# A new list of steps for the stick-breaking stage, with the adaptive weights visited four tiles at a time

## The chip, the cores and the metric

The kernel runs on one core of a Trainium2 chip. The metric is the device time of one execution in microseconds (us). The time before is 1705.46 us, the median of 3 runs (1704.63 to 1706.43). One execution was profiled; it took 1706.82 us, and its span from first to last instruction is 1704.7 us.

Engine names: PE is the matmul engine (PEld its weight loads), ACT the scalar engine, DVE the vector engine, POOL the general engine, which here mostly issues stores, and SP the engine that issues loads. PE, ACT and DVE each work through their own instructions in the order in which the program lists them; they meet at semaphores only.

## The reference, cut

One layer of a hybrid encoder for 1024 prompt frames and 32 sample frames, in float32. The part that the change touches is the stick-breaking attention (8 heads of 64) and the matmuls that run beside it: the gate projections and the adaptive (ada) vectors.

```python
ada = jax.nn.silu(c) @ w_ada + b_ada            # 1024 -> 6 * 1024, for two rows c
sh1, sc1, gt1, sh2, sc2, gt2 = split(ada, 6)
h = rms_norm(x, g_pre_mix) * (1 + sc1) + sh1
p = h @ w_in                                     # 4256 columns, 2048 of them the two gates
...
def sb_attend(q, qpos, k, v, kpos):
    z = einsum('bqhd,bshd->bhqs', q, k) * SB_SCALE
    mask = kpos[None, :] < qpos[:, None]
    sp = where(mask, softplus(z), 0.0)
    later = cumsum(sp, axis=3, reverse=True) - sp
    a = where(mask, exp(log_sigmoid(z) - later), 0.0)
    return einsum('bhqs,bshd->bqhd', a, v)
...
x = x + gt1 * rms_norm(merged @ w_out, g_post_mix)
h2 = rms_norm(x, g_pre_ffn) * (1 + sc2) + sh2
```

`sh1` and `sc1` are needed before the projection and are made in the first stage. The other four vectors of `ada` (32 weight tiles of 128x1024) are made inside the stick-breaking stage, since nothing needs them sooner.

## The kernel before

The stages follow each other: normalised input (`stage_h`), the q, k, v projections (`stage_qkv`), stick-breaking attention (`stage_sb`), latent projections (`stage_lat`), latent attention, merge, up and down projections. The change lies in `stage_sb`, which the trace shows from 193.01 to 516.87 us.

`stage_sb` makes four passes (`for p in range(4)`, at the end of `stage_sb`), one for each pair of heads. In a pass `sb_attend` walks the list `ORDER` (L691 to L711), written out by hand: each entry issues one piece of work, and the entries of PE, ACT and DVE go to these engines in just that order (`manual_schedule`). So the list decides what stands behind what on each engine. The same list serves all four passes.

An entry is a letter and a place, as in `S2.0a`: here 2 is the unit (four units of 256 query rows for each of two heads, 0 to 7), 0 the first of its two blocks of 128 rows, and a or b the half of the key columns where they are too many for one PSUM bank. The letters:

- `S` (PE): the scores, two matmuls (L1154, L1155) into one of three PSUM banks called `s`.
- `a`, `e`, `l` (ACT): absolute value, exp, log of the scores (L742, L744, L746). `x`, `c`, `k`, `d` (DVE): softplus, the running sum along the keys (a scan, L752 or L755), a copy of its first column, the difference (L748 to L760). `d` is the last to read the bank, so a later `S` in that bank waits for it. `E` (ACT, L762): the final exp.
- `T` (PE, L803): transposes of the weights into one of two banks `tr`; `h` (ACT) and `v` (DVE) copy them out in two parts; `V` (PE, L817): the product with the values; `o` (ACT) and `p` (DVE) copy the result out.
- `f` (PE): the next step of the gate projections, which fill PE while the attention waits for ACT and DVE. Such a step is three matmuls of 128x352 (L75, L76, L77). Eight steps make one block of a gate tile in one of two PSUM banks `mm`, three blocks make a tile, 16 tiles make the gates: four tiles, 96 steps, in each pass.
- `G` (ACT): copy a finished block out of its `mm` bank (L1080); POOL then stores it. `W` (ACT, L68) and `w` (DVE, L71): split the next gate tile's weights in two parts; `W` waits until the load of that tile (`wr`) has landed. The load of tile m+1 is issued when tile m begins.
- `D`, `Q` (DVE): add the ada products to their sum; turn a finished vector.

The ada products are made in `ada_step`. Before, a visit takes two weight tiles and follows the first block of every gate tile (L1064 to L1067), each weight tile being one step `f` of the list; so a pass has 104 `f`, of which 8 are ada tiles. A weight tile takes four matmuls (L236), one for each group of 32 columns of PE's array, into one `mm` bank:

```python
for j in range(4):
    nc.tensor.matmul(ps[32 * j : 32 * j + 32, :256], self.cT[:, k], w[:, j * 256 : j * 256 + 256], ...)
```

After a visit `ada_fetch` issues the loads of the next one's weight tiles. The loads of a pass's q, k and v (`queries`, `values`) are issued beside certain entries (the dictionary `then`: the second head's at `S2.0a` and `S2.1a`, the next pass's first head at `S3.1b` and `V3.0`). All these loads and those of the gate weights go through SP's queue (`load`, L83) in the order of the program. The stores of `stage_qkv` go through POOL's queue and are still under way when `stage_sb` begins.

Of the kernel before, what the change touches and what calls it, by code (L numbers as in the profile page):

```python
# [8 lines left out]
F32 = mybir.dt.float32  # L9
# [8 lines left out]
P = 128  # L18
D = 1024
# [25 lines left out]
class K:  # L45
# [182 lines left out]
    def ada_step(self, n, pool, tp, late):  # L228


        nc, a = self.nc, self.a
        ps = self.bank("mm")
        for i, (v, k) in enumerate(self.ada_todo[:n]):
            w = self.ada_w.pop(0)
            for j in range(4):
                nc.tensor.matmul(ps[32 * j : 32 * j + 32, :256], self.cT[:, k], w[:, j * 256 : j * 256 + 256],  # L236
                                 start=i == 0, stop=i == n - 1)
# [10 lines left out]
        yield  # L248

    def ada_turn(self):  # L250

# [192 lines left out]
    def stage_qkv(self):  # L444
# [249 lines left out]
        f2 l1.1 x2.0a V0.0 E1.0 c2.0a f1 a2.0b o0 f1 x1.1 e2.0b f1 W p0 f1 k2.0a d2.0a l2.0b f1 c1.1 E2.0a f1  # L694
        S2.1a x2.0b G f1 a2.1a d1.1 e2.1a c2.0b f2 E1.1 f1 w l2.1a S2.1b f1 a2.1b x2.1a T1.1 e2.1b T1.0 d2.0b
        h1.1 c2.1a f1 h1.0 f1 l2.1b v1.1 S3.0a E2.0b v1.0 f1 a3.0a f1 k2.1a d2.1a G e3.0a x2.1b V1.1 E2.1a c2.1b
        l3.0a S3.0b V1.0 x3.0a a3.0b o1 f1 p1 T2.2 h2.2 e3.0b d2.1b f1 c3.0a f1 E2.1b f1 l3.0b v2.2 S3.1a k3.0a
        d3.0a T2.1 h2.1 a3.1a x3.0b E3.0a V2.2 f1 c3.0b T2.0 e3.1a S3.1b h2.0 f1 v2.1 l3.1a f1 G v2.0 a3.1b f1
        x3.1a W f1 d3.0b V2.1 c3.1a D V2.0 f1 w o2 S4.0 e3.1b E3.0b f1 a4.0 f1 l3.1b f1 p2 e4.0 k3.1a d3.1a l4.0
        f2 x3.1b E3.1a f1 x4.0 c3.1b f1 G T3.3 c4.0 S4.1 a4.1 T3.2 h3.3 d3.1b f1 e4.1 v3.3 h3.2 f1 d4.0 f1 l4.1  # L700
        E3.1b v3.2 S5.0 f1 E4.0 x4.1 c4.1 a5.0 V3.3 e5.0 V3.2 l5.0 d4.1 T3.1 E4.1 x5.0 T3.0 h3.1 f1 c5.0 h3.0
        S5.1 S6.0a v3.1 a5.1 f1 v3.0 a6.0a T4.0 e5.1 f1 d5.0 h4.0 V3.1 E5.0 v4.0 f1 l5.1 V3.0 G x5.1 S6.0b e6.0a
        f1 o3 c5.1 f1 a6.0b l6.0a e6.0b f1 p3 l6.0b d5.1 f2 x6.0b E5.1 V4.0 x6.0a f1 o4 c6.0a S6.1a T5.1 p4
        a6.1a T5.0 k6.0a d6.0a h5.1 f1 c6.0b e6.1a f1 G h5.0 v5.1 f1 E6.0a v5.0 S6.1b l6.1a f1 W f1 x6.1a d6.0b
        V5.1 V5.0 D c6.1a E6.0b a6.1b S7.0a w o5 f2 e6.1b l6.1b a7.0a f1 k6.1a p5 e7.0a f1 d6.1a x6.1b E6.1a f1
        c6.1b l7.0a S7.0b f1 x7.0a T6.2 a7.0b f1 d6.1b h6.2 c7.0a f1 E6.1b f1 G e7.0b S7.1a v6.2 f1 k7.0a d7.0a
        l7.0b T6.1 T6.0 a7.1a h6.1 V6.2 x7.0b c7.0b h6.0 S7.1b e7.1a f1 v6.1 E7.0a f1 v6.0 l7.1a f1 d7.0b a7.1b
        f1 x7.1a V6.1 E7.0b V6.0 e7.1b c7.1a f1 G o6 l7.1b f1 p6 k7.1a d7.1a x7.1b f2 E7.1a f1 c7.1b f2 T7.3
        d7.1b T7.2 h7.3 f1 h7.2 E7.1b v7.3 f1 G f1 v7.2 f1 V7.3 V7.2 D T7.1 f1 h7.1 v7.1 T7.0 f1 h7.0 v7.0 f1
        V7.1 f2 V7.0 f1 o7 f1 W p7 f1 Q f1 w G f7 G  # L710
    """.split()  # L711

    def sb_attend(self, score, V, out, fill, then):
        nc = self.nc
        act, vec = nc.scalar.activation, nc.vector
        tiles, banks, seen = {}, {}, {}
        common = self.sums(V, out, tiles)
        todo = None
        for x in self.ORDER:
            if todo:  # L720
                todo()
            todo = then.get(x)
            k, x = x[0], x[1:]
            if k in "fGDQWw":
                for _ in range(int(x or 1)):
                    fill(k)
                continue
            h, u = divmod(int(x[0]), 4)
            if k in "SaelxckdE":
                n, i, part = x[0], int(x[2]), x[3:]  # L730
                w = (2 * u + i + 1) * P
                m = w // 2 if part else w
                c0 = m if part == "a" else 0
                if k == "S":
                    if part != "b":
                        tiles[x[:3]] = self.tl(self.At, [P, TP], F32, "A")
                    banks[x] = self.tl(self.ps, [P, 512], F32, "s")
                    score(h, banks[x], 2 * u + i, c0, max(m, 256))
                    continue
                ps, A = banks[x][:, :m], tiles[x[:3]][:, c0 : c0 + m]  # L740
                if k == "a":
                    act(A, ps, AF.Abs)  # L742
                elif k == "e":
                    act(A, A, AF.Exp, scale=-1.0)  # L744
                elif k == "l":
                    act(A, A, AF.Ln, bias=1.0)  # L746
                elif k == "x":
                    vec.scalar_tensor_tensor(A, ps, 0.0, A, ALU.max, ALU.add)  # L748
                elif k == "c":
                    r = A[:, ::-1]  # L750
                    if part == "b":
                        vec.tensor_tensor_scan(r, r, r, seen[x[:3]], ALU.add, ALU.bypass)  # L752
                    else:

                        vec.tensor_tensor_scan(r, self.reset[:, 512 - m : 512][:, ::-1], r, -NEG, ALU.mult, ALU.add)  # L755
                elif k == "k":
                    seen[x[:3]] = self.tl(self.sm, [P, 1], F32, "mn")
                    vec.tensor_copy(seen[x[:3]], A[:, 0:1])
                elif k == "d":
                    vec.tensor_tensor(A, ps, A, ALU.subtract)  # L760
                else:
                    act(A, A, AF.Exp)  # L762
                continue
            common(k, x, h, u)
# [278 lines left out]
    def gates(self):  # L1043
# [7 lines left out]
        def steps():  # L1051
            for m in range(16):
                wh, wl = w.pop(0)
                for b, (c0, n) in enumerate(self.BLK):
                    if b == 0:
                        c = 2208 + (m + 1) * P if m < 15 else 3 * P
                        raw.append(self.wload([(0, 1024, self.a["w_in"][0, :, c : c + P].rearrange("(k p) c -> p k c", p=P), 8)]))
                    ps.append((m, c0, n, self.bank("mm")))
                    for k in range(KT):
                        self.mm3(ps[-1][3][:, :n], wh[:, k], wl[:, k], self.Hh[k][:, c0 : c0 + n],  # L1060
                                 self.Hl[k][:, c0 : c0 + n], k == 0, k == KT - 1)
                        if k < KT - 1:
                            yield
                    if b == 1 and self.ada_sum is not None:  # L1064
                        ada.append(self.ada_turn())
                    yield
                    if b == 0:  # L1067
                        yield from self.ada_step(2, self.sm2, self.Sp, ada)
                        if m == 15:
                            self.sample_load(1)  # L1070

        step = steps()

        def do(kind):
            if kind == "f":
                next(step)
            elif kind == "G":
                m, c0, n, x = ps.pop(0)
                g = self.tl(self.At, [P, 512], F32, "nat")
                nc.scalar.copy(g[:, :n], x[:, :n])  # L1080
# [25 lines left out]
    def stage_sb(self):  # L1106
# [1500 lines left out]
```

## Time and profile before

| what | value |
|---|---|
| median of 3 runs | 1705.46 us |
| the profiled execution, its span | 1706.82 us, 1704.7 us |
| PE busy, DVE busy, ACT busy over the span | 97%, 75%, 58% |
| `stage_sb`, first pass | 85.64 us |
| `stage_sb`, second to fourth pass | 79.41, 79.40 and 79.41 us |
| instructions of `stage_sb` on PE in a pass | some 556 |

A group's row gives line, engine, operation, what is written and read, shape, count, then busy time, mean duration and the idle time before it with what ended it. A timeline row gives the start in us from the span's start, the duration, then the same names; idle time before it stands in brackets. PE's matmuls overlap: a matmul of 128x352 lasts 0.32 us, but the next one starts 0.16 us later, so the cost of a step on PE is the time from start to start.

### The profile page before, as it was taken

Reading aid. Unit: us, or ns where it says so; the run is one execution under the profiler, and the core shown is the slowest. Engines: PE = TensorE matmul, PEld = TensorE weight load, DVE = VectorE, ACT = ScalarE, POOL = GpSimd, SP = SyncE. Lnnn points to the kernel's source line nnn. Section 1 sums busy time; section 2 is a strip of 40 time slices with the busy share of each in tenths; the row PEclk is TensorE's granted clock in tenths of the full one; section 3 lists DMA queues with packets and bytes.
Section 4 is the critical chain, followed back from the end, with each engine's and each line's share of the span. In section 5 each row is a group of like instructions: output and inputs, shape, how many; then the busy total and the mean of one; then the engine's idle time right before and its main releaser. Section 6 shows DMA issues by size and latency. Waiting matters only on the chain. (4 is left out here: it accounts for less than half of the span.)

```text
span 1704.7 us, 30268 instructions
## 1 busy us (share of the span) xinstructions
PE 1660.8 (97%) x11646; PEld 1512.1 (89%) x11646; DVE 1272.9 (75%) x2129; ACT 993.6 (58%) x1945; POOL 292.8 (17%) x569
## 2 busy tenths in 40 slices
PE   5999999999999999999999999999999999999997
PEld 3999889999999898998889789999999999887885
DVE  4865697979783688777766779887787777787456
ACT  4544597978774667777763476444444444544442
POOL 3113311111110221111100221221121111110013
PEclk8999999999999999999999999999999999999999
DMA  9345984647432421222374531433333333697643
GB/s 333 100 133 180 280 250 130 200 117 227 150 104 66 149 79 47 67 68 70 107 238 140 173 131 62 134 104 131 131 104 132 131 108 133 231 331 250 207 139 120
DMA packets 185728, 255.20 MB, mean 150 GB/s; under 512 B 14702, under 2 KB 125056, under 8 KB 185584
## 3 DMA queue, kind: packets, MB, share of 16 engines
q1 hardware_dynamic: 164944, 194.11, 36.5%
q0 software_dynamic: 20416, 59.08, 9.8%
q8 instruction: 91, 1.49, 0.4%
q14 instruction: 53, 0.43, 0.1%
q10 hardware_dynamic: 224, 0.09, 0.0%
HBM read 187.86 MB, written 64.57 MB: 148 GB/s over the span
## 5 line engine op out<-in xcount | busy, mean ns | idle before, releaser
L68 ACT ACTIVATE wh<-wr 128x1024 fp32r<-128x1024 f32 (+5 forms) x163 | 132.2, 820 | 226.3 <-PE s L2061 80.4
L71 DVE TENSOR_TENSOR wl<-wr,wh 128x1024 fp32r<-128x1024 f32 (+5 forms) x163 | 149.9, 928 | 78.0 <-ACT wh L68 77.6
L75 PE MATMUL mm<-hh,wh 128*128 128x352 f32 x456 | 153.0, 336 | 0.0
L76 PE MATMUL mm<-hl,wh 128*128 128x352 f32 x456 | 149.5, 328 | 0.4 <-DVE hl L331 0.3
L77 PE MATMUL mm<-hh,wl 128*128 128x352 f32 x456 | 148.7, 326 | 0.0
L2060 PE MATMUL mm<-T,wh 128*128 128x256 f32 (+1 forms) x376 | 108.1, 288 | 0.0
L2062 PE MATMUL mm<-T,wl 128*128 128x256 f32 (+1 forms) x376 | 107.0, 285 | 0.3 <-DVE wl L71 0.2
L2061 PE MATMUL mm<-T,wh 128*128 128x256 f32 (+1 forms) x376 | 106.7, 284 | 0.0
L2060 PE MATMUL s<-T,wh 128*128 128x256 f32 (+1 forms) x348 | 99.2, 285 | 0.0
L2062 PE MATMUL s<-T,wl 128*128 128x256 f32 (+1 forms) x348 | 99.1, 285 | 0.0
L2061 PE MATMUL s<-T,wh 128*128 128x256 f32 (+1 forms) x348 | 99.0, 284 | 0.0
L71 DVE TENSOR_TENSOR wl<-S,wh 128x1024 fp32r<-128x1024 f32 (+1 forms) x55 | 59.1, 1077 | 49.2 <-ACT wh L68 48.8
L76 PEld LDWEIGHTS mm<-hl,wh 128*128 128x128 f32 x456 | 86.4, 190 | 3.3 <-DVE hl L331 1.8
L75 PEld LDWEIGHTS mm<-hh,wh 128*128 128x128 f32 x456 | 86.4, 190 | 3.2 <-ACT A L762 1.6
L2201 DVE SCALAR_TENSOR_TENSOR u<-u,c,u 128x1058 f32<-128x1058 f32 x68 | 87.0, 1316 | 2.0 <-ACT u L2198 0.7
L77 PEld LDWEIGHTS mm<-hh,wl 128*128 128x128 f32 x456 | 86.5, 190 | 0.2
L803 PE MATMUL tr<-c,A 128*128 128x128 f32 x576 | 84.2, 275 | 0.9 <-DVE A L919 0.3
L68 ACT ACTIVATE wh<-S 128x1024 fp32r<-128x1024 f32 (+1 forms) x55 | 51.8, 943 | 49.5 <-PE s L2061 13.4
L2062 PE MATMUL tr<-T,wl 128*128 128x272 f32 (+1 forms) x272 | 77.6, 285 | 0.2 <-DVE wl L71 0.2
L2060 PE MATMUL tr<-T,wh 128*128 128x272 f32 (+1 forms) x272 | 77.7, 286 | 0.0
L2061 PE MATMUL tr<-T,wh 128*128 128x272 f32 (+1 forms) x272 | 77.3, 284 | 0.0
L71 DVE TENSOR_TENSOR PTl<-tr,PTh 128x512 fp32r<-128x512 f32 x96 | 64.5, 683 | 13.1 <-ACT PTh L68 12.3
(760 smaller groups left out, 5789.2 us busy)
## 6 DMA issues: line engine op xcount, KB each, us to landing
wr<-in_w_up_dram SPq DMA_DIRECT2D x44, 512.0 KB, 4.0
dr<-in_w_down_dram SPq DMA_DIRECT2D x43, 512.0 KB, 5.9
wr<-in_w_in_dram SPq DMA_DIRECT2D x33, 512.0 KB, 5.4
A<-in_w_ada_dram SPq DMA_DIRECT2D x32, 512.0 KB, 7.6
wr<-gdn SPq DMA_DIRECT2D x30, 512.0 KB, 5.0
gdn<-u POOLq DMA_DIRECT2D x23, 512.0 KB, 5.1
gd<-nat POOLq DMA_DIRECT2D x48, 176.0 KB, 4.1
t<-gd SPq DMA_DIRECT2D x16, 528.0 KB, 5.6
```

What stands on the lines that cost most here:

```text
L68: self.nc.scalar.activation(out, in_, AF.Identity, scale=scale)
L71: return self.nc.vector.tensor_tensor(out, full, hi.bitcast(F32), ALU.subtract)
L75: m(ps, lh, rh, start=start, stop=False)
L76: m(ps, lh, rl, start=False, stop=False)
L77: self.pe = m(ps, ll, rh, start=False, stop=stop).ins
L803: self.nc.tensor.transpose(tr[:, (2 * s + q) * P : (2 * s + q + 1) * P], at[q][:, b * P : b * P + P], self.idt)
L2060: m(ps[:, :n], w[0][:, k], x[0][:, k, c], start=first and k == 0, stop=False, skip_group_check=True)
L2061: m(ps[:, :n], w[0][:, k], x[1][:, k, c], start=False, stop=False, skip_group_check=True)
L2062: i = m(ps[:, :n], w[1][:, k], x[0][:, k, c], start=False, stop=k == 3, skip_group_check=True)
L2201: nc.vector.scalar_tensor_tensor(y, u[:, w : w + YW], self.cvT[:, w, cc : cc + 1], y, ALU.mult, ALU.add)
```

## The change

The list `ORDER` is written anew: the same entries of the attention, with other places; 96 `f` in place of 104, two `D` in place of four, and two new entries `A`. The `f` stand closer together at a pass's start and are gone from its end. Its first lines, some from a quarter of the way down, and the last, before and now:

```diff
-        S0.0 S0.1 a0.0 S1.0 a0.1 e0.0 e0.1 l0.0 f2 l0.1 x0.0 a1.0 x0.1 f1 c0.1 c0.0 e1.0 f1 l1.0 f1 d0.0 d0.1
-        E0.0 f1 x1.0 c1.0 E0.1 f1 S1.1 S2.0a a1.1 T0.0 d1.0 f1 G a2.0a h0.0 v0.0 f1 e2.0a f1 e1.1 S2.0b l2.0a D
+        S0.0 a0.0 f1 S0.1 f1 a0.1 e0.0 S1.0 f1 l0.0 f1 e0.1 f1 a1.0 l0.1 e1.0 f1 x0.0 c0.0 f1 d0.0 E0.0 f2 S2.0a
+        x0.1 c0.1 f1 l1.0 f1 a2.0a x1.0 d0.1 c1.0 W f1 e2.0a f1 G l2.0a w x2.0a f1 S1.1 f1 a1.1 f1 E0.1 f2 e1.1
...
-        h1.1 c2.1a f1 h1.0 f1 l2.1b v1.1 S3.0a E2.0b v1.0 f1 a3.0a f1 k2.1a d2.1a G e3.0a x2.1b V1.1 E2.1a c2.1b
-        l3.0a S3.0b V1.0 x3.0a a3.0b o1 f1 p1 T2.2 h2.2 e3.0b d2.1b f1 c3.0a f1 E2.1b f1 l3.0b v2.2 S3.1a k3.0a
+        l2.1b h1.0 c2.1a E2.0a f2 S3.0a x2.1b T1.1 G a3.0a h1.1 k2.1a e3.0a d2.1a f4 v1.0 E2.1a S3.0b l3.0a f1
+        c2.1b f2 v1.1 x3.0a d2.1b V1.1 c3.0a G a3.0b f1 e3.0b S3.1a l3.0b x3.0b E2.0b E2.1b T2.2 k3.0a d3.0a A
+        h2.2 c3.0b V1.0 v2.2 a3.1a d3.0b f1 e3.1a S4.0 l3.1a T2.0 f1 W x3.1a S3.1b o1 T2.1 D E3.0a a3.1b c3.1a G
+        f1 p1 f2 e3.1b f2 w a4.0 f2 k3.1a d3.1a S5.0 h2.1 l3.1b x3.1b V2.2 h2.0 E3.1a f1 e4.0 v2.1 a5.0 T3.3
...
-        V7.1 f2 V7.0 f1 o7 f1 W p7 f1 Q f1 w G f7 G
+        d7.0b h7.3 d7.1b E7.0b f3 E7.1b f1 v7.3 p6 f1 v7.2 T7.1 V7.3 V7.2 h7.1 T7.0 f1 G f1 h7.0 f1 w G v7.1
+        v7.0 V7.1 V7.0 o7 p7
```

An `A` is one visit of four ada tiles at once; two in a pass, so beside every second gate tile. `ada_step` is no longer a generator, and the gates' steps no longer call it:

```diff
             for j in range(4):
                 nc.tensor.matmul(ps[32 * j : 32 * j + 32, :256], self.cT[:, k], w[:, j * 256 : j * 256 + 256],
                                  start=i == 0, stop=i == n - 1)
-            if i < n - 1:
-                yield
...
-            if k in "fGDQWw":
+            if k in "fGDQWwA":
...
                     yield
-                    if b == 0:
-                        yield from self.ada_step(2, self.sm2, self.Sp, ada)
-                        if m == 15:
-                            self.sample_load(1)
...
+            elif kind == "A":
+                self.ada_step(4, self.sm2, self.Sp, ada)
+                if not self.ada_todo:
+                    self.sample_load(1)
```

The first ada tiles are no longer loaded ahead of the first pass, but four at once beside `S2.1a` of the first pass; the buffers of the pool `sm2` are laid out ahead:

```diff
+        for g, w, n in (("big", BIG, 3), ("A", TP, 2)):
+            for _ in range(n):
+                self.tl(self.sm2, [P, w], F32, g)
 
         self.sent = self.wlast
         queries(0, 0)
-        self.ada_w = []
-        self.ada_fetch(2, S)
+        self.ada_w, self.ada_sum = [], None
         values(0, 0)
...
             then = {"S2.0a": lambda: queries(p, 1), "S2.1a": lambda: values(p, 1)}
+            if p == 0:
+                then["S2.1a"] = lambda: (values(p, 1), self.ada_fetch(4, self.sm2))
```

Outside `stage_sb` the three engines' instructions stand as before. Three places where they moved follow, each as the program's own list of instructions before and after (an x4 at a row's end counts equal ones; the changed kernel's line numbers are a few lower).

The first place is PE at the ada visit in the middle of the second pass before, where `A` are the ada weight tiles, `mm` a PSUM bank, `s` scores:

```order
L77 MATMUL mm_2789<-hh_94,wl_2586 128x352
L236 MATMUL mm_2864<-A_2592,cT 32x256 x4
L1154 MATMUL s_2871<-KH_279_2205,Q_278_2204 128x384
L1155 MATMUL s_2871<-KL_277_2203,Q_278_2204 128x384
L236 MATMUL mm_2864<-A_2594,cT 32x256 x4
L75 MATMUL mm_2886<-hh_94,wh_2585 128x352
```

And the first visit of the first pass now:

```order
L800 MATMUL tr_2536<-c_70,A_2387 128x128
L236 MATMUL mm_2543<-A_2392,cT 32x256 x4
L236 MATMUL mm_2543<-A_2394,cT 32x256 x4
L236 MATMUL mm_2543<-A_2396,cT 32x256 x4
L236 MATMUL mm_2543<-A_2398,cT 32x256 x4
L814 MATMUL pv_2514<-PTh_2448,V_285_2216 128x256
```

Two weight tiles that stood apart, or in pairs elsewhere, are now four in a row.

The second place is ACT in the first pass, at the split of the first gate tile that the stage loads (`wh<-wr`, the entry `W`). Before, it is ACT's 24th instruction of the stage and stands behind the first product's copy (`o<-pv`):

```order
L762 ACTIVATE A_2245<-A_2245 128x384
L742 ACTIVATE A_2295<-s_2335 128x320
L789 COPY o_2360<-pv_2349 64x256
L744 ACTIVATE A_2295<-A_2295 128x320
L68 ACTIVATE wh_2370<-wr_2253 128x1024
L746 ACTIVATE A_2295<-A_2295 128x320
```

Now it is the 12th:

```order
L759 ACTIVATE A_2237<-A_2237 128x128
L743 ACTIVATE A_2257<-A_2257 128x384
L739 ACTIVATE A_2292<-s_2293 128x320
L68 ACTIVATE wh_2315<-wr_2242 128x1024
L741 ACTIVATE A_2292<-A_2292 128x320
L1073 COPY nat_2325<-mm_2244 128x352
```

The split moved up by twelve instructions; the copy of the first gate block (`nat<-mm`), which stood well ahead of it, is now behind it.

The third place is SP's queue at the stage's start, before:

```order
L83 DMA KL_286_2217<-kl_546 64x1024 x2
L83 DMA A_2229<-in_w_ada_dram 128x1024
L83 DMA A_2231<-in_w_ada_dram 128x1024
L83 DMA V_285_2216<-vd_550 128x8x128
L83 DMA wr_2253<-in_w_in_dram 128x8x128
L83 DMA Q_278_2204<-qh_534 64x1024
```

And now, from the same place to the next gate tile's load:

```order
L83 DMA KL_286_2217<-kl_546 64x1024 x2
L83 DMA V_285_2216<-vd_550 128x8x128
L83 DMA wr_2242<-in_w_in_dram 128x8x128
L83 DMA Q_278_2204<-qh_534 64x1024
...
L83 DMA V_276_2202<-vd_550 128x8x128
L83 DMA A_2392<-in_w_ada_dram 128x1024
L83 DMA A_2394<-in_w_ada_dram 128x1024
L83 DMA A_2396<-in_w_ada_dram 128x1024
L83 DMA A_2398<-in_w_ada_dram 128x1024
L83 DMA wr_2417<-in_w_in_dram 128x8x128
```

The two ada tiles that stood ahead of the gate tile's load are gone from there, and four stand ahead of the next one.

More of the change, by code (lines that the diff above doesn't have):

```diff
@@ L247, in ada_step @@
         self.ada_sum = v if k == KT - 1 else None
-        yield
     def ada_turn(self):
@@ L697 @@
-        l3.0a S3.0b V1.0 x3.0a a3.0b o1 f1 p1 T2.2 h2.2 e3.0b d2.1b f1 c3.0a f1 E2.1b f1 l3.0b v2.2 S3.1a k3.0a
[L698 to L706, printed above, removed]
@@ new lines @@
+        x0.1 c0.1 f1 l1.0 f1 a2.0a x1.0 d0.1 c1.0 W f1 e2.0a f1 G l2.0a w x2.0a f1 S1.1 f1 a1.1 f1 E0.1 f2 e1.1
+        f1 l1.1 d1.0 S2.0b c2.0a x1.1 G T0.0 a2.0b f1 h0.0 e2.0b k2.0a d2.0a l2.0b f2 S2.1a v0.0 E1.0 f1 c1.1
+        V0.0 x2.0b d1.1 f1 a2.1a f1 e2.1a l2.1a c2.0b x2.1a d2.0b f1 S2.1b o0 E1.1 p0 a2.1b f1 T1.0 e2.1b f1
+        l2.1b h1.0 c2.1a E2.0a f2 S3.0a x2.1b T1.1 G a3.0a h1.1 k2.1a e3.0a d2.1a f4 v1.0 E2.1a S3.0b l3.0a f1
+        c2.1b f2 v1.1 x3.0a d2.1b V1.1 c3.0a G a3.0b f1 e3.0b S3.1a l3.0b x3.0b E2.0b E2.1b T2.2 k3.0a d3.0a A
@@ new lines @@
+        h2.2 c3.0b V1.0 v2.2 a3.1a d3.0b f1 e3.1a S4.0 l3.1a T2.0 f1 W x3.1a S3.1b o1 T2.1 D E3.0a a3.1b c3.1a G
+        f1 p1 f2 e3.1b f2 w a4.0 f2 k3.1a d3.1a S5.0 h2.1 l3.1b x3.1b V2.2 h2.0 E3.1a f1 e4.0 v2.1 a5.0 T3.3
+        e5.0 V2.1 l4.0 v2.0 c3.1b V2.0 f1 T3.2 h3.3 f1 l5.0 v3.3 E3.0b o2 d3.1b f1 S4.1 f1 x4.0 h3.2 p2 G f1
+        V3.3 E3.1b T3.1 a4.1 c4.0 e4.1 v3.2 V3.2 x5.0 T3.0 d4.0 l4.1 S5.1 c5.0 f1 x4.1 f1 d5.0 h3.1 S6.0a h3.0
+        f1 v3.1 a5.1 v3.0 e5.1 f1 l5.1 a6.0a c4.1 E4.0 x5.1 f4 e6.0a V3.1 d4.1 l6.0a S6.0b E4.1 T4.0 E5.0 c5.1
@@ new lines @@
+        x6.0a f1 d5.1 f1 W f1 S6.1a G a6.0b c6.0a h4.0 w k6.0a e6.0b f1 d6.0a l6.0b E5.1 v4.0 V3.0 a6.1a f2
+        S6.1b o3 x6.0b p3 f1 e6.1a c6.0b l6.1a f1 V4.0 T5.1 f1 a6.1b o4 x6.1a f1 e6.1b d6.0b c6.1a S7.0a G l6.1b
+        f1 x6.1b k6.1a d6.1a f1 c6.1b h5.1 a7.0a f1 v5.1 f1 T5.0 S7.1a E6.0a f2 G e7.0a f1 d6.1b p4 E6.1a l7.0a
+        a7.1a h5.0 e7.1a S7.0b f1 x7.0a v5.0 f1 V5.1 T6.2 c7.0a f1 a7.0b l7.1a f1 V5.0 x7.1a k7.0a e7.0b d7.0a
+        h6.2 c7.1a f1 E6.1b l7.0b v6.2 x7.0b f1 k7.1a c7.0b S7.1b f1 E6.0b o5 f1 G a7.1b T6.1 d7.1a p5 T6.0
@@ L711 @@
+        e7.1b h6.1 h6.0 v6.0 A D l7.1b v6.1 f1 V6.2 f1 V6.1 x7.1b E7.0a W Q E7.1a T7.2 h7.2 c7.1b T7.3 V6.0 o6
+        d7.0b h7.3 d7.1b E7.0b f3 E7.1b f1 v7.3 p6 f1 v7.2 T7.1 V7.3 V7.2 h7.1 T7.0 f1 G f1 h7.0 f1 w G v7.1
+        v7.0 V7.1 V7.0 o7 p7
     """.split()
```

5 lines of the change are left out of this document (removed).

## The prediction

> **What bounds the kernel now.** After the page's busy shares (97% on PE) I read the table by stretches, one stretch for each pass, and then the timelines of PE, ACT, DVE and SP.
>
> ```profile
> 193.01:278.65 85.64, 81.11 (x558) 73.95 (x556) 71.00 (x123) 64.95 (x143) 20.76 (x41) 0.98 0.84 253
> 278.65:358.06 79.41, 78.83 (x556) 72.87 (x555) 67.43 (x117) 64.00 (x140) 12.95 (x24) 1.00 0.57 169
> ...
> 200.07:203.48 3.41, 3.41 (x18) 2.58 (x22) 2.03 (x4) 1.46 (x5) 1.69 (x4) 0.50 1.06 411
> ```
>
> The columns are the stretch, its length, busy time of PE, PEld, DVE, ACT and POOL with counts, then the granted clock, the DMA share and GB/s. The stage is four passes of one list. In the later ones PE is busy for all but 0.6 of 79.41 us, and DVE and ACT have 12 and 15 us to spare: PE bounds them. The matmuls of the attention and of the gates are the same before and after, so a pass can only lose what PE spends on switching to the ada tiles and what it waits. The first pass is 6.23 us longer than the others; the last row shows PE at half clock for 3.41 us of it.
>
> **The ada visits.** A pair of weight tiles and a single one, on PE in the second pass:
>
> ```profile
> 284.25 0.32 PE L77 MATMUL mm<-hh,wl 128*128 128x352 f32 x1
> 284.50 1.07 PE L236 MATMUL mm<-A,cT 128*32 128x256 f32 x16
> 285.50 0.42 PE L1154 MATMUL s<-KH,Q 128*128 128x320 f32 x1
> 285.75 0.31 PE L1155 MATMUL s<-KL,Q 128*128 128x320 f32 x1
> 285.90 0.32 PE L75 MATMUL mm<-hh,wh 128*128 128x352 f32 x1
> 325.78 0.32 PE L77 MATMUL mm<-hh,wl 128*128 128x352 f32 x1
> 326.03 0.64 PE L236 MATMUL mm<-A,cT 128*32 128x256 f32 x8
> 326.60 0.44 PE L1154 MATMUL s<-KH,Q 128*128 128x384 f32 x1
> ```
>
> Around a pair the start to start from L77 to the score is 1.25 us; 0.16 of it is the gate matmul's own. The score's first matmul then takes 0.25 where its equal twin takes 0.15, so a pair costs 1.09 + 0.10 = 1.19. The single costs 0.82 - 0.16 + 0.10 = 0.76. A weight tile is therefore worth 0.43, and a visit 0.33 on top, whatever its length. Before, a pass makes five visits (three pairs, and one pair that the list cuts in two): 3 x 1.19 + 2 x 0.76 = 5.09. Now two visits of four: 2 x (0.33 + 4 x 0.43) = 4.10. That is -0.99 in a pass, -4.0 in all. No row shows four tiles in a row. Bounds: if each tile cost what the single costs, 6.08 (+1.0 in a pass); if a visit cost nothing beyond its tiles, 3.44 (-1.65). I take the pair's price, the nearest row. The two `D` that fall away are on DVE, which has time to spare: nothing.
>
> **The waits of a later pass.** PE's longest waits there are for a score bank, which `d` on DVE must free; the first row is the longest. The other rows are prices: one product, four transposes, ACT's and PE's work on a score of 512 columns, and the copy of a gate block.
>
> ```profile
> 376.81 0.47 PE L1154 MATMUL s<-KH,Q 128*128 128x448 f32 x1 [0.34 <-DVE A L760]
> 375.84 0.63 PE L817 MATMUL pv<-ptd,V 128*128 128x256 f32 x4
> 348.31 0.60 PE L803 MATMUL tr<-c,A 128*128 128x128 f32 x4
> L742 ACT ACTIVATE A<-s 128x512 f32<-128x512 f32 x18 | 10.8, 599 | 0.3
> L1080 ACT COPY nat<-mm 128x352 f32<-128x352 f32 x36 | 16.2, 450 | 14.6 <-PE mm L77 14.5
> L1155 PE MATMUL s<-KL,Q 128*128 128x512 f32 x18 | 7.1, 394 | 0.0
> ```
>
> A wait costs its idle time and the 0.16 us by which a running matmul outlasts its place in the row. With 0.58 idle and some four waits, that is 1.2 us in a pass, and no list can win more than this here. The wait shown, 0.34 + 0.16 = 0.50, is that of `S3.0b`, whose bank is freed by `d2.1a`. Between `S3.0a` and `S3.0b` PE had two gate steps (three matmuls, 0.48, each) and one product (four matmuls, 0.48 from start to start), 1.4 us; now it has the three transposes of `T1.1` and four gate steps, 2.2 us. So that wait should go.
>
> A new one comes. The first `A` takes one of the two `mm` banks, so the third block of the running gate tile must wait for the copy `G` of the second. That copy stands on ACT behind `a3.1b`, which waits for the score `S3.1b`. From the start of that score's second matmul: 0.39 to its end, some 0.48 to 0.60 for `a3.1b`, 0.45 for the copy and 0.1 for hand-overs make 1.4 to 1.5; PE has that matmul's 0.23 from start to start and four transposes to do, 0.60 less the last one's overrun of 0.16: 0.67 in all. PE waits 0.75 to 0.85. Everything on PE queues behind it. The new list's waits are then between 0.75 (all old ones gone) and 1.95 (all kept); I take 0.9, near the low end since the one that I can follow goes. That is -0.3 in a pass. No trailing `f` covers the pass's end now: `V7.1` and `V7.0` come behind a weight split, `v7.1` and `v7.0` on DVE, which I take as part of the 0.15 left.
>
> **The first pass: a score's wait.** Before, PE lost three times here: it waited for a score bank, then ran at half clock, and then waited again, because ACT waited for the gate weights' load.
>
> ```profile
> 199.94 0.64 PE L1154 MATMUL s<-KH,Q 128*128 128x512 f32 x1 [2.49 <-DVE A L760]
> 212.71 0.44 PE L1154 MATMUL s<-KH,Q 128*128 128x384 f32 x1 [1.36 <-DVE A L760]
> 210.12 1.06 ACT L68 ACTIVATE wh<-wr 128x1024 fp32r<-128x1024 f32 x1 [2.59 <-DMA wr<-in_w_in_dram]
> 211.09 0.45 ACT L746 ACTIVATE A<-A 128x320 f32<-128x320 f32 x1
> 211.45 0.45 ACT L762 ACTIVATE A<-A 128x320 f32<-128x320 f32 x1
> ```
>
> Their sum is 2.65 + 3.41/2 + 1.52 = 5.9 of the 6.23. Now the first tile's chain runs through alone (`x0.0 c0.0 d0.0`).
>
> ```profile
> 197.81 0.61 DVE L748 SCALAR_TENSOR_TENSOR A<-s,A 128x128 f32<-128x128 f32 x2
> L748 DVE SCALAR_TENSOR_TENSOR A<-s,A 128x128 f32<-128x128 f32 x6 | 1.7, 285 | 12.2 <-ACT A L746 12.2
> L755 DVE TENSOR_TENSOR_SCAN A<-reset,A 128x128 f32<-128x128 bf16 x6 | 2.4, 399 | 0.0
> L760 DVE TENSOR_TENSOR A<-s,A 128x128 f32<-128x128 f32 x6 | 1.7, 284 | 0.1
> 193.01 0.36 PE L1154 MATMUL s<-KH,Q 128*128 128x256 f32 x1
> 193.91 0.32 PE L75 MATMUL mm<-hh,wh 128*128 128x352 f32 x1
> ```
>
> DVE cannot begin before 197.81, since the previous stage holds it; 0.29 + 0.40 + 0.28 and some 0.1 for hand-overs end at 198.85, so the fourth score (`S2.0a`) starts at 198.9. PE gets there at 193.01 + 0.90 for three scores + 9 steps x 0.48 = 198.24. It waits 0.66, not 2.65.
>
> **The first pass: the gate weights.** The split `W` stands twelve instructions earlier on ACT, which reaches it at about 199.7 instead of 207.5. Its load will not be there.
>
> ```profile
> 186.31 0.86 SPq L83 DMA_DIRECT2D A<-in_w_ada_dram  x2
> 187.28 0.58 SPq L83 DMA_DIRECT2D V<-vd  x1
> 187.98 1.90 SPq L83 DMA_DIRECT2D wr<-in_w_in_dram  x1
> q0 software_dynamic: 1039, 3.28, 72.2%
> q1 hardware_dynamic: 2006, 1.14, 34.6%
> ```
>
> The last two rows are the DMA queues from 195.2 to 206.5: q0 is POOL's stores of the stage before, q1 the loads, here the values and the gate weights (1024 packets each), held to 178 packets per us by the stores. The two ada tiles that stood ahead kept q1 from 192.0 to 195.2; without them the two loads start 3.2 us sooner. At the same pace they land at 210.1 - 3.2 = 206.9. In those 3.2 us, though, q1 had 47% of the engines (q0's 54% being the other row of that stretch):
>
> ```profile
> q0 software_dynamic: 187, 0.70, 54.3%
> q1 hardware_dynamic: 220, 0.58, 46.8%
> ```
>
> Packets of these loads take 34.6% x 11.3 / 2006 = 1.95 ns of all engines each, so 1.5 us hold up to 770, and 1236 are left: 195.2 + 6.9 = 202.1 if the tail behind the last packet vanished, 205.7 if it stays 3.6 us (206.5 to 210.1). I take 205.5; the ends are 202 and 210.1.
>
> What is queued behind the split: on ACT `e2.0a`, then the copy of the first gate block. PE needs that copy's bank for its 17th gate step. It gets there at 198.9 + 0.30 (the score of 320 columns, 2 x 0.15) + 7 x 0.48 + 0.46 (`S1.1`, 512 columns) = 203.0. The copy is done 0.97 + 0.36 + 0.45 + 0.1 = 1.9 us after the landing (211.09 - 210.12, 211.45 - 211.09, the copy's 450 ns): 207.4. PE waits 4.4 us. The wait of 2.49 before was followed by 3.41 us at half clock, that of 1.36 was not; so this one will be, for 1.7 us. In all the first pass pays 0.66 + 4.4 + 1.7 + the 0.3 left over of before = 7.1 against 6.23: +0.9.
>
> The Trainium skill (TensorE: Matmul & The Clock Gate, What's actually happening) says that the clock drops after an idle window of 3413 ns, and that these windows run freely. The trace agrees on the length (3.41 us), but there an idle stretch of 2.49 us was enough, so the measurement decides. By a rule of a whole idle window the 4.4 us need not hold one, and the time would be 1.7 us less.
>
> **The ada tiles of the first pass.** Four tiles, 2 MB, now stand ahead of the second gate tile's load. Ahead of them are 2 MB of q, k and v.
>
> ```profile
> 206.57 3.88 SPq L83 DMA_DIRECT2D A<-in_w_ada_dram  x2
> 212.33 4.63 SPq L83 DMA_DIRECT2D wr<-in_w_in_dram  x1
> 206.50:212.00 5.50, 4.85 (x31) 4.56 (x29) 3.41 (x8) 2.86 (x7) 2.59 (x5) 1.00 1.03 199
> 216.00:224.00 8.00, 7.65 (x52) 7.13 (x51) 7.86 (x16) 7.28 (x18) 1.08 (x2) 1.00 0.92 287
> ```
>
> At 199 to 287 GB/s 4 MB from 205.5 land between 219.5 and 225.6. PE is at the first `A` after 22 gate steps (10.6), 13 transposes (1.4), 8 products (1.0) and 6 scores (2.2) from 207.4, with the half clock at about 224.3. I cost it at nothing; its cover is these 15 us.
>
> **The sum.** Passes two to four: 3 x (-0.99 - 0.3) = -3.9. First pass: -0.99 - 0.3 + 0.9 = -0.4. Together -4.3: the span goes from 1704.7 to 1700.4, and the median, 0.8 us above the span, from 1705.46 to about 1701.1. What follows the stage starts earlier and is the same.
>
> **The rivals.** The weights land early, by 203: PE resumes at 204.9, waits 1.9 and keeps its clock, since 1.36 did not cost it; 2.5 + 1.7 less, 1696.9. For it: the 1.5 us of free engines above; against it: the 3.6 us tail. No half clock at all: 1699.4; against it stands the row of 200.07. The weights land as late as before, 210.1, because the stores set the pace: 4.6 more, 1705.7. The list wins nothing in a later pass and the bank wait comes on top: +0.75 in place of -0.3, four times, 1705.3; for it, that I followed only one old wait. On the other side, the ada tiles arrive late: the visit waits on PE for all four. Landing at 233, the wait is 8.7 and the half clock 1.7: 1711.5. It decides from about 230.5 on. For it: SP's queue stood for 4 to 5 us at a time there (the rows of 206.57 and 212.33); against it: the two rates.
>
> **How the numbers follow.** Forecast 0.47, own range 1699 to 1703; early weights 0.17; no half clock 0.08; late weights 0.10; list without gain 0.10; late ada tiles 0.08. A measurement of this kernel tells 0.2% (3.4 us) from no change, so faster is below 1702.05 and slower above 1708.87. Faster: four fifths of the forecast, the early weights, and the kept clock, 0.63; same: 0.28; slower: late ada tiles and a little more, 0.09. The range reaches from the early weights to the late ones: 1696.5 to 1706.
>
> **What would show it.** Right: 32 rows of L236 in a visit take 2.05 us from the L77 or L803 ahead to the next operation; passes two to four take about 78.1 us; ACT waits 5 to 6 us for `wr` at about 200 and PE 4 to 5 at about 203, with a half clock behind. Wrong: PE waiting for an ada tile's DMA, a later pass over 79 us, a wait on PE at a pass's end, or no wait for `wr`.

## The result, and the profile after

The change made the kernel faster: 1695.8 us (median of 4 runs, 1694.53 to 1697.87) against 1705.21 us, a ratio of 0.9945 with a 95% interval of 0.9928 to 0.9962. The profiled execution took 1697.87 us, the slowest of the four; its span is 1696.0 us where the prediction's sum came to 1700.4 and before had 1704.7. So the gain is 8.7 us of span where 4.3 were forecast.

The table by stretches, one for each pass of the changed kernel and one behind the stage; the columns are those of the prediction's first fence:

```profile
193.59:276.12 82.53, 78.81 (x557) 74.97 (x555) 69.19 (x120) 65.18 (x143) 19.77 (x40) 0.98 0.77 245
276.12:352.69 76.57, 76.57 (x556) 73.41 (x555) 66.14 (x115) 64.14 (x140) 13.56 (x25) 1.00 0.60 169
352.69:429.26 76.57, 76.57 (x557) 73.41 (x555) 66.24 (x116) 64.14 (x140) 11.01 (x20) 1.00 0.65 179
429.26:505.83 76.57, 76.57 (x557) 73.41 (x556) 66.23 (x116) 64.15 (x140) 13.09 (x24) 1.00 0.48 143
505.83:540.00 34.17, 33.45 (x212) 31.25 (x211) 10.54 (x27) 14.80 (x33) 2.19 (x4) 0.95 0.18 53
```

Read the second number against the first: in the later passes PE is busy for all of 76.57 us, where before it was busy for 78.83 of 79.41. A later pass is 2.84 us shorter (forecast 1.29), the first 3.11 shorter (forecast 0.4): 11.6 us in the stage. Some 2.9 us of that are missing from the span: the stage begins 0.58 us later in this execution (193.59, before 193.01), PE runs at half clock for 3.41 us behind the stage (the 0.95 of the last row, 1.7 us), and 0.6 are spread over the rest. The first two come and go between executions: over the twelve profiled kernels of this document the stage begins between 191.49 and 193.86 us, and four of them have a half clock at that place. Nothing ties them to the change.

The ada visit in a later pass, on PE's timeline:

```profile
300.36 0.49 PE L800 MATMUL tr<-c,A 128*128 128x128 f32 x3
300.78 1.93 PE L236 MATMUL mm<-A,cT 128*32 128x256 f32 x32
302.64 0.38 PE L814 MATMUL pv<-PTh,V 128*128 128x256 f32 x1
302.87 0.28 PE L814 MATMUL pv<-PTl,V 128*128 128x256 f32 x1
```

The 32 rows take 1.86 us from start to start, and the product behind them 0.23 where its twins take 0.12. The transposes ahead hand on some 0.1 late (0.42 us; three of them take 0.25 at 218.18, in front of a gate matmul that is itself 0.08 slower). Together that is the 2.05 of the forecast.

The first pass: PE's two waits, from its timeline,

```profile
199.60 0.39 PE L1153 MATMUL s<-KH,Q 128*128 128x320 f32 x1 [0.60 <-DVE A L757]
...
207.09 0.43 PE L75 MATMUL mm<-hh,wh 128*128 128x352 f32 x1 [3.12 <-ACT nat L1073]
```

and ACT's timeline at the same place:

```profile
200.50 1.05 ACT L68 ACTIVATE wh<-wr 128x1024 fp32r<-128x1024 f32 x1
201.46 0.46 ACT L741 ACTIVATE A<-A 128x320 f32<-128x320 f32 x1
206.58 0.45 ACT L1073 COPY nat<-mm 128x352 f32<-128x352 f32 x1 [4.66 <-DMA qh<-T]
```

PE stands at the very gate step that the prediction named, but not for the reason it gave. The split `W` (200.50) waits for nothing. It is the copy `G` behind it that waits, 4.66 us, for a store to land: the trace names the store of `qh`, on POOL's queue. The reading is that the copy's buffer `nat` lies over memory from which `qh` is still being stored; e3 tests it.

### The profile page after: what moved, and what is told of

Its sections match the earlier page's. It is cut to its first block, busy times and chain, and to the rows that moved or that the text cites. A ratio compares the mean times of both kernels' runs of the same rounds, so it can differ in the third digit from the quotient of the medians.

```text
span 1696.0 us, 30259 instructions
## 1 busy us (share of the span) xinstructions
PE 1654.6 (98%) x11646; PEld 1516.9 (89%) x11646; DVE 1268.3 (75%) x2121; ACT 996.1 (59%) x1945; POOL 295.1 (17%) x569
## 5 line engine op out<-in xcount | busy, mean ns | idle before, releaser
L2192 POOL COPY c<-u 128x2 f32<-128x2 f32 x44 | 26.9, 611 | 266.1 <-DVE u L2138 230.1
```

## The experiments

All kernels below compute the same as the changed one. Times are medians. They come from several chips, and each ratio is to runs of the kernel before on the same chip (1705.2 to 1707.6 us), so compare ratios across rows, not times. The pass lengths are from the one profiled execution of each and are the finer measure, since a half clock more or less moves a run by 1.7 us.

| kernel | time, us | ratio to before (95%) | first pass | later passes |
|---|---|---|---|---|
| before | 1705.21 | | 85.64 | 79.41 |
| changed | 1695.80 | 0.9945 (0.9928 to 0.9962) | 82.53 | 76.57 |
| e1, old list, new visits | 1713.38 | 1.0041 (1.0026 to 1.0056) | 88.07 | 81.33, 80.69 |
| e2, new list, visits of two | 1696.92 | 0.9946 (0.9931 to 0.9961) | 83.15 | 77.37 |
| e3, copy's buffers moved | 1697.65 | 0.9952 (0.9935 to 0.9969) | 84.51 | 76.57 |
| e4, changed once more | 1697.99 | 0.9938 (0.9926 to 0.9951) | 82.52 | 76.56 |
| e5, four buffers | 1692.18 | 0.9912 (0.9898 to 0.9925) | 78.19 | 76.57 |
| e6, and a first list | 1692.14 | 0.9906 (0.9890 to 0.9922) | 79.72 | 76.57 |
| e7, one visit of eight | 1705.48 | 0.9986 (0.9977 to 0.9995) | 90.67 | 77.11 |
| e8, ada tiles ahead of the values | 1693.91 | 0.9918 (0.9903 to 0.9933) | 79.87 | 76.57 |
| e9, and another first list | 1694.52 | 0.9920 (0.9904 to 0.9937) | 80.21 | 76.57 |
| e10, a late `D` | 1698.27 | 0.9945 (0.9928 to 0.9961) | 82.54 | 77.40 |

### e1: the old list with the new visits

What the visits are worth without the new list. In the list of before the eight `f` and two of the `D` that belong to the pairs fall away, and `A` stands where the second and the fourth pair began:

```diff
-        G v2.0 a3.1b f1 x3.1a W f1 d3.0b
+        G v2.0 a3.1b A x3.1a W d3.0b
...
-        v7.3 f1 G f1 v7.2 f1 V7.3
+        v7.3 f1 G A v7.2 V7.3
```

> The list of before with its places, but two visits of four weight tiles in a pass, and the loads as the change has them. If the visits are worth what the prediction gave them and the rest of the gain is the list's, a later pass takes 79.41 - 0.99 = 78.4 us and the whole run 1699 to 1701. If the visits carry the whole gain of a later pass (2.84 us), it takes 76.6 and the run is level with the changed kernel (1696). First pass: the gate weights should now have landed well before their split is reached, so ACT's wait of 2.59 for them goes and PE's wait of 1.36 with it; PE's wait of 2.49 for a score bank stays.

Neither came: a later pass is 1.3 to 1.9 us longer than before. PE's waits in the second pass of e1 (waiting tile, what it waited for, total, times, longest):

```profile
PE s L1151 <- DVE A L755: 1.3, 3, 0.5
PE pv L812 <- DVE ptd L71: 0.2, 1, 0.2
```

Before, 0.58 us of idle time stood in the whole pass, 0.34 of it at the one score bank that the prediction shows; here it is 1.82. Idle time is only part of it. Counted from start to start, ten places of this pass are late by 3.5 us, and the instructions that waited there take another 1.0 more than their twins; before, the same count gives 1.8. That is 2.7 more; less the 1.0 that the visits save it makes 1.7 of the 1.9. The new waits stand right behind the places that lost a pair. The first:

```profile
287.53 0.41 PE L1151 MATMUL s<-KH,Q 128*128 128x320 f32 x1 [0.48 <-DVE A L755]
```

This is the score that the prediction shows behind a pair, at 285.50. So in the old list the pairs were themselves cover: DVE and ACT worked while PE was at the weight tiles, at places where a score bank was about to come free. The two parts of the change do not add up; here visits of four paid only with a list that brings gate steps to those places. The other expectation held in part: with the loads of the change `W` of the first pass waits for nothing here either. But a wait stands first among ACT's in that pass that before does not have:

```profile
ACT nat L1071 <- DMA qh<-T: 4.2, 1, 4.2
```

It is the one of the changed kernel's first pass, and the second `qh` store takes 9.8 us from issue to landing here as it does there (before: 6.5). So it comes with the loads, not with the list.

### e2: the price of a visit

The new list, four visits of two tiles. The two further ones:

```diff
-        f1 p1 f2 e3.1b f2 w a4.0 f2 k3.1a
+        f1 p1 f2 e3.1b f1 A f1 w a4.0 f1 D f1 k3.1a
...
-        c6.1a S7.0a G l6.1b f1 x6.1b
+        c6.1a S7.0a G A l6.1b f1 D x6.1b
...
-                self.ada_step(4, self.sm2, self.Sp, ada)
+                self.ada_step(2, self.sm2, self.Sp, ada)
```

and each visit's loads go out two visits ahead.

> The new list, with four visits of two weight tiles in a pass in place of two of four (the first new place behind the 44th gate step, the other behind the 71st). If a visit costs 0.33 us beside its tiles, a later pass takes 76.57 + 0.66 = 77.2 us and the run is 2.6 us longer than the changed kernel (1698.4). If a visit costs nothing beside its tiles, a later pass stays at 76.6; if a tile alone were cheaper in a row of four, more than 77.2.

```profile
274.83:352.20 77.37, 77.37 (x557) 73.10 (x555) 66.37 (x117) 64.32 (x140) 13.49 (x25) 1.00 0.59 171
```

This row of e2's second pass shows PE busy throughout, as in the changed kernel, and 0.80 us more. That would be 0.40 for each further visit, against 0.33 in the prediction. But a short wait is mixed into it, behind the third visit; the first row is DVE's `D`, the second PE's next gate block:

```profile
329.76 0.42 DVE L242 TENSOR_TENSOR ada<-ada,mm 128x256 f32<-128x256 f32 x1 [2.15 <-PE mm L236]
330.24 0.43 PE L75 MATMUL mm<-hh,wh 128*128 128x352 f32 x1
```

`D` ends at 330.18, just as PE gets to the block, and the block's first matmul takes 0.26 us to the next start where its twins take 0.16, as matmuls behind a wait do. Less these 0.1 a visit costs some 0.35, as forecast. The run's time does not show the difference (ratio 0.9946 against 0.9945). In the profiles e2's stage begins 1.9 us earlier and has no half clock behind it, and a difference of this size is lost in such things.

### e3: where the first pass's wait comes from

```diff
-        for g, w, n in (("PTh", 512, 2), ("PTl", 512, 2), ("o", 256, 2), ("nat", 512, 2)):
+        for g, w, n in (("PTh", 512, 2), ("nat", 512, 2), ("PTl", 512, 2), ("o", 256, 2)):
```

> The changed kernel with the buffers of the gate blocks' copies (nat) laid 6144 bytes lower, over memory whose last store lands at about 197, and PTl and o in their place. If the 3.1 us that PE waits in the first pass comes from the copy's buffer, which the last qh store still reads, the wait and the half clock behind it go: first pass 82.5 to about 77.5 us, run about 1691. If it comes from the gate weights' load or from the crowded DMA engines as such, the first pass stays at 82 to 83 and the run at 1695.8. If another wait stands right behind, the first pass lies between.

ACT's timeline in e3's first pass:

```profile
201.39 0.44 ACT L1073 COPY nat<-mm 128x352 f32<-128x352 f32 x1
...
206.16 0.45 ACT L1073 COPY nat<-mm 128x352 f32<-128x352 f32 x1 [1.46 <-DMA qh<-T]
...
217.98 0.45 ACT L1073 COPY nat<-mm 128x352 f32<-128x352 f32 x1 [4.48 <-DMA gd<-nat]
```

The first copy now runs at 201.39 without a wait, so the buffer was the cause. The second still waits 1.46 us for the `qh` store. The third waits 4.48 us, and PE 3.7 with it: it needs the first one's buffer back, and the store of that (`gd<-nat`) is issued only at 210.65, 9 us after the copy. POOL issues in its list's order, and ahead of it stand small loads into buffers of the ada sums, which wait for the stores of the stage before:

```profile
209.19 1.47 POOL L226 DMA_DIRECT2D ada<-in_b_ada_dram  x3 [0.72 <-DMA ql<-fq]
210.65 1.12 POOL L1074 DMA_DIRECT2D gd<-nat  x2
```

The pass is 2 us longer than the changed kernel's. The wait moved and grew by 0.6, and the half clock behind it lasts longer (granted clock of the pass 0.96, in the changed kernel 0.98).

### e4 to e6: enough buffers, and then the next limit

e5 gives the copies four buffers of the width that they use; e6 also gives the first pass its own list (`ORDER0`), with two `f` more ahead of `S2.0a`. e4 is the changed kernel again, on the chip of these runs.

```diff
-        for g, w, n in (("PTh", 512, 2), ("PTl", 512, 2), ("o", 256, 2), ("nat", 512, 2)):
+        for g, w, n in (("PTh", 512, 2), ("nat", 352, 4), ("PTl", 512, 2), ("o", 256, 2)):
             for _ in range(n):
-                self.tl(S, [P, w], F32R if g[0] == "P" else F32, g)
+                self.tl(S, [P, w], F32R if g[0] == "P" else F32, g, n)
...
-                g = self.tl(self.At, [P, 512], F32, "nat")
+                g = self.tl(self.At, [P, 352], F32, "nat", 4)
```

> The changed kernel once more, on the chip of the three runs that follow, as their measure: 1694 to 1698 us, later passes 76.57. If the two half clocks of its profile (at 207.8 behind PE's wait of 3.1 us, and at 532 in the latent stage, whose instructions are those of before) are decided by where a fixed grid of 3.413 us windows happens to fall, they need not come again at the same places; if they belong to the kernel, they do.

> The changed kernel with four buffers for the gate blocks' copies (352 columns each) in place of two, the first over memory that is free by 197. If both the wait of the changed kernel (3.1 us) and the one that took its place when the two buffers were moved (3.7 us, for the store of the first copy) are waits for a free buffer and for nothing else, both go, with their half clock: first pass about 77.5 us, run some 5 us below the changed kernel (1690 to 1692). If the stores of POOL's queue hold something else as well, the first pass stays above 80.

> As the run before, and in the first pass alone two gate steps stand ahead of S2.0a instead of behind E0.1, so that DVE's late start (it is held by the stage before until 197.8) is covered: PE's wait of 0.76 us there goes, first pass about 76.7 us, run 0.7 us below the run before. If the two steps are missed where they were, a wait of up to 0.96 us appears between S1.1 and S2.0b and nothing is won.

The first pass of e5 by stretches, and its waits on PE:

```profile
193.67:271.86 78.19, 77.37 (x558) 73.42 (x556) 68.99 (x120) 65.05 (x143) 19.79 (x40) 1.00 0.80 259
```

```profile
PE s L1153 <- DVE A L757: 0.6, 1, 0.6
PE pv L814 <- DVE ptd L71: 0.2, 1, 0.2
```

PE's waits for the copies are gone and the clock stays at 1.00: 4.3 us less in the first pass. On the same chip e5 takes 1692.18 us where the changed kernel takes 1697.99; this version beats the kernels before and after. In e6 the wait at `S2.0a` goes too, and PE's list of waits in the first pass begins with another:

```profile
PE mm L236 <- DMA A<-in_w_ada_dram: 1.2, 1, 1.2
```

PE reaches the first visit before the weight tiles do. The run is level with e5 within its interval, and the profiled pass is 1.5 us longer. So e5 already stands at the edge where the loads of the first pass take over.

### e7: one visit of eight, and a load that is late

In the list of e5 the first `A` and its `D` fall away, and `ada_step(8, ...)` stands at the second; the first eight tiles are asked for where the four were; three of the eight tiles lie in the buffers `big`, which the stage does not use.

> As the run with four buffers, but one visit of eight weight tiles in a pass, at the second place, and none at the first. If a visit costs 0.40 us beside its tiles, as the run with four visits of two has it, a later pass takes 76.57 - 0.40 = 76.2 us. If the list needs the first visit as cover for ACT and DVE at that place (1.7 us of PE's work are gone there), scores or transposes wait and the pass is longer than 76.57.

```profile
191.49:282.16 90.67, 79.83 (x557) 75.65 (x555) 69.03 (x119) 64.94 (x143) 19.79 (x40) 0.94 0.71 234
282.16:359.27 77.11, 76.98 (x557) 73.48 (x556) 65.67 (x114) 64.06 (x140) 13.53 (x25) 1.00 0.60 170
```

A later pass is 0.54 us longer, not 0.4 shorter. Within 9 us behind the place where the first visit stood PE is held up three times: by 0.12 us each ahead of two scores (308.98 and 313.50, both just as DVE's `d` ends) and by 0.29 ahead of transposes (315.20). With what the instructions behind take longer that is 0.8, and the visit saved makes up some 0.3 of it. So the first visit was cover, as in e1. The first pass is 12.5 us longer than e5's. ACT's and PE's timelines say why:

```profile
230.64 1.06 ACT L68 ACTIVATE wh<-wr 128x1024 fp32r<-128x1024 f32 x1 [10.51 <-DMA wr<-in_w_in_dram]
```

```profile
234.51 0.69 PE L1151 MATMUL s<-KH,Q 128*128 128x384 f32 x1 [10.05 <-DVE A L755]
```

With eight tiles (4 MB) ahead of it on SP's queue, the next gate tile's load lands late, `W` waits 10.5 us for it, and ACT's whole queue behind it, until PE stands 10 us for a score bank; a half clock adds to it (granted clock of the pass 0.94). This is the chain that the prediction put at the stage's start: it exists, but needs a load that is late, and there it was not.

### e8 and e9: asking for the tiles earlier

e8 is e5 with the two calls of the first pass swapped; e9 adds a list of its own for the first pass, with its two steps taken from behind `V0.0`.

```diff
-                then["S2.1a"] = lambda: (values(p, 1), self.ada_fetch(4, self.sm2))
+                then["S2.1a"] = lambda: (self.ada_fetch(4, self.sm2), values(p, 1))
```

> The run with four buffers, and in the first pass the four weight tiles are asked for ahead of the second head's values instead of behind them (SP's queue stood from 195 to 206.9 for the values' buffer, which the qh stores hold). The visit of the first pass did not wait in the run with four buffers, so by the theory that PE alone bounds the pass nothing changes (first pass 78.2 us, run 1692), unless the 2 MB that come earlier delay the qh stores and the scores' loads behind them: then the first pass is longer.

> As the run before, with a list of its own for the first pass: two gate steps stand ahead of S2.0a, taken from behind V0.0 instead of from behind E0.1. PE's wait of 0.76 us at S2.0a goes, the weight tiles are there in time (they were 1.2 us late with the first such list), first pass about 77.4 us, run 0.8 us below the run before. If the tiles are late all the same, PE waits at the first visit and nothing is won.

Neither gained: the first pass takes 79.87 and 80.21 us in the one profile of each, in e5 78.19 (the run times, ratios 0.9918 and 0.9920, can't be told from e5's). So e8 is longer, though not for the reason given, and e9 missed. SP issues the tiles at 209.2, in e5 at 209.7: hardly sooner. What holds SP until then is a store, again of the stage before; its own wait in e8:

```profile
SPq L83 <- DMA ql<-fq: 14.0, 1, 14.0
```

The values' load, which in e5 goes out at 206.9, ahead of that wait, now goes out at 211.2, between the tiles and the gate tile's load, and the gate tile lands later (its split starts at 224.65, in e5 at 222.98). ACT's waits in e8's first pass:

```profile
ACT PTh L68 <- PE tr L800: 3.2, 4, 1.6
ACT wh L68 <- DMA wr<-in_w_in_dram: 3.2, 1, 3.2
ACT nat L1073 <- DMA qh<-T: 1.3, 1, 1.3
```

### e10: the bank wait, forced

```diff
-        T2.1 D E3.0a a3.1b c3.1a G f1 p1 f2 e3.1b f2 w a4.0
+        T2.1 E3.0a a3.1b c3.1a G f1 p1 f2 e3.1b f2 w D a4.0
```

> The changed kernel with the first D of a pass some eight entries later on DVE, behind w, so that the ada products' mm bank comes free after the copy G, and the gate block that follows the first visit takes the bank which G frees. That is the wait of the prediction: if its arithmetic holds, PE waits 0.75 to 0.85 us there in every pass, and a later pass takes 76.57 + 0.8 = 77.4 us (run 3.2 us above the changed kernel). If ACT is in truth early enough there, the pass stays at 76.6, and then the prediction's size was wrong as well as its bank.

PE and ACT in e10's second pass, on their timelines:

```profile
305.50 0.43 PE L75 MATMUL mm<-hh,wh 128*128 128x352 f32 x1 [0.59 <-ACT nat L1071]
```

```profile
304.50 0.60 ACT L737 ACTIVATE A<-s 128x512 f32<-128x512 f32 x1 [0.51 <-PE s L1152]
305.00 0.45 ACT L1071 COPY nat<-mm 128x352 f32<-128x352 f32 x1
```

0.59 idle and the 0.16 by which the matmul ahead outlasts its row are 0.75, and the pass is 0.83 longer (77.40). The size that the prediction gave this wait was right to the tenth; it only did not apply to the changed kernel. There the bank comes from `D`, on DVE's timeline of the changed kernel:

```profile
303.83 0.41 DVE L242 TENSOR_TENSOR ada<-ada,mm 128x256 f32<-128x256 f32 x1
```

It is done at 304.24; the gate block that needs a bank begins at 305.69, ahead of the copy `G`, which runs from 306.03 on without anyone waiting for it.

## Why the prediction was right in sign and too small in size

- **PE bounds the passes.** Right, and more so after: no idle time is left in a later pass.
- **The ada visits, -0.99 in a pass.** Right: 2.05 for a visit of four as the rows above have it, and some 0.35 for a visit beside its tiles as e2 has it (0.33 forecast). But it is worth that only in the new list (e1).
- **The waits of a later pass, -0.3.** This is the step that failed; it was -1.8 (2.84 less the visits). Two of its terms were wrong. The old waits were to go in part, and "no list can win more than this here" put them at 1.2 us together. All of them went, and they were worth 1.8. Counted from start to start in the second pass before, the four waits cost 1.22, as the sum has it. The instructions that had waited then cost 0.33 more, which the sum left out; here the score that waited and its equal twin, 0.31 and 0.19 to the next start:

```profile
297.39 0.47 PE L1154 MATMUL s<-KH,Q 128*128 128x448 f32 x1 [0.34 <-DVE A L760]
297.70 0.36 PE L1155 MATMUL s<-KL,Q 128*128 128x448 f32 x1
297.89 0.28 PE L817 MATMUL pv<-PTh,V 128*128 128x256 f32 x1
```

  And 0.23 stand at two hold-ups that show no idle time (301.65 and 310.53). The second wrong term is the 0.9 us of new waits, which did not come; most of it was the `mm`-bank wait of 0.75 to 0.85. The text took the block behind the visit to need the bank that `G` frees. It gets the visit's own, which `D` frees 1.5 us before it is wanted. e10 shows the size right and the bank wrong. Four passes times 1.55 us are 6.2 of the 7.3 us by which the stage was misjudged; the first pass's own waits, put at 7.1 and in truth 6.0, are the rest.
- **The first pass: a score's wait.** Right: 0.60 + 0.16 = 0.76, forecast 0.66.
- **The first pass: the gate weights.** The place was right (the 17th gate step), the half clock behind it too (207.79 to 211.20), the size near (3.12 idle and 0.16 make 3.28 us, forecast 4.4), and the cause wrong. That a wait of about that size stood at that step all the same is luck. The load `wr` was put at 205.5, with 202 as its lower end. It landed at 199.8. Its row, of the loads issued between 184.5 and 185.5 in the changed kernel (KB, us from issue to landing):

```profile
wr<-in_w_in_dram SPq DMA_DIRECT2D x1, 512.0 KB, 14.6
```

  The failed step here is the count of what moves early. The prediction gave the loads the 3.2 us between 192.0 and 195.2 that the ada tiles had used. In truth the two loads fill the loads' queue from 185.2 on, while the stores are still light. The same queue from 185.2 to 193.9, before:

```profile
q1 hardware_dynamic: 558, 1.95, 66.4%
```

  and in the changed kernel (packets, MB, share of the engines):

```profile
q1 hardware_dynamic: 1621, 1.75, 76.0%
```

  Some 1060 packets more in that stretch, as many as half of the 2048 of the two loads. The stores pay for it. SP also gets through the second head's loads sooner (the last is issued at some 195, before at some 203), and they run beside the stores. From 195.2 to 206.5 the stores (q0) moved 3.28 MB before, as the prediction shows, and in the changed kernel:

```profile
q0 software_dynamic: 779, 2.69, 59.6%
q1 hardware_dynamic: 1070, 1.85, 43.4%
```

  The second `qh` store, issued at some 196 to 197 in both, before and in the changed kernel:

```profile
qh<-T POOLq DMA_DIRECT2D x1, 512.0 KB, 6.5
```

```profile
qh<-T POOLq DMA_DIRECT2D x1, 512.0 KB, 9.8
```

  It lands at some 206.5 in place of 202.6, and that is what the copy's buffer waits for. Nothing in the prediction asked what lies under the buffers that the moved copy writes. e1 shows that the late store comes with the loads, e3 and e5 that the buffer is what waits. Which of the loads slows the store was not tried apart.
- **The ada tiles of the first pass cost nothing.** Right for the changed kernel (no wait at its first visit, 224.2). The cover was thinner than the 15 us it was given: with the other waits gone, e6 finds the tiles 1.2 us late.
- **Half clock.** The Trainium skill (TensorE: Matmul & The Clock Gate, What's actually happening) has the clock fall after an idle window. By that rule the 3.28 us would have kept the clock, and the pass would be 1.7 us shorter. The trace does not agree, and neither did the one before: in the window of 3.41 us ahead of the drop PE was busy for 0.70 us (204.38 to 207.79), and before for 0.92 (196.66 to 200.07).
- **The rivals.** Early weights came true as a mechanism (the load landed at 199.8), and their time, 1696.9, is near the result by luck: PE's wait, which they were to end at 204.9, lasted until 207.1 for another reason, and the time came from the list. The list without gain and the late weights fell; late ada tiles did not come here, and did once the other waits were gone (e6).

## What to carry to other kernels

Before a wait is charged to a moved instruction, ask which buffer it reuses and who frees that one. Here the gate block took the PSUM bank that came free first, not the one that the prediction had in mind; and the copy's inputs were there in time, only the old content under its output was not yet stored. Extra work on the bounding engine can be cover for the others, so a saving there is worth its price only where the order closes the gap. When loads move up in a queue, ask which stores then come later, and who waits for the memory that these read.

## What the runs showed of the hardware

The half clock follows a fixed grid of windows, and the same instructions fall under it in one execution and not in another. In the changed kernel the half clock at 532.06 starts 95 windows of 3.413 us behind the one at 207.79. The window ahead of it and the one that it takes:

```profile
528.64:532.06 3.42, 2.85 (x22) 2.54 (x22) 1.46 (x6) 0.60 (x2) 0.57 (x1) 1.00 0.02 5
532.06:535.47 3.41, 3.41 (x14) 3.41 (x13) 0.00 (x0) 1.07 (x2) 0.54 (x1) 0.50 0.05 12
```

Before, the same stretch lies otherwise in the grid of that execution. It begins (539.05 on PE's timeline) 1.06 us behind a window's start, in the changed kernel (527.96) 0.68 us ahead of one, and the clock stayed:

```profile
537.99:541.40 3.41, 2.84 (x22) 2.66 (x21) 0.90 (x3) 0.95 (x2) 0.27 (x1) 1.00 0.00 0
541.40:544.82 3.42, 3.42 (x26) 3.29 (x26) 0.56 (x3) 1.07 (x2) 0.80 (x2) 1.00 0.04 10
```

The first row of each has PE busy for 83%, and only one of the two cost the clock. That one holds 13 matmuls of 64 columns and 7 of 128; the other holds 14 of 64 and 6 of 352. So the busy time of the profile does not decide it, and a window that is busy for 2.85 of 3.42 us can cost the clock; what is counted stays open. In e4, the same kernel, there was none at 532; it came at 863.5 instead, 192 windows behind the one of its first pass (208.19). Such a half clock is worth 1.7 us, a fifth of this change's whole gain, and comes and goes between executions of one kernel.
